# Nine pairs of an attention layer issued by another timing table, and one helper moved to the head of the queue for free slots

## The chip, the cores and the metric

The kernel runs on one core of one Trainium2 chip. The metric is device time in microseconds (us), the median of several runs; lower is better. A core has five engines that run side by side, each through its own instructions in the order in which they were issued: PE (TensorE, matrix products; its weight loads are listed apart as PEld), DVE (VectorE), ACT (ScalarE), POOL (GpSimd) and SP (SyncE, which here issues all transfers). They wait for each other through semaphores.

## The reference, cut to what matters

The reference is a two-layer transformer on 1024 latent and 256 context tokens, width 1024, 16 heads of 64. The change touches only layer 0's attention. For each head, every latent token attends to an 8 by 16 neighbourhood of the 16 by 64 grid, with a bias by relative position, and to all 256 context tokens, in one softmax; context tokens attend to the context tokens alone. The results of all heads are multiplied by `w_o`, scaled by a gate and added to the input:

```python
s_nb = q_r . k_b * scale + bias ; s_nb = where(col_in, s_nb, -1e30)
s_cx = q_r . kc * scale
p = softmax(concat([s_nb, s_cx]))
o = p[..., :n_nb] @ v_b + p[..., n_nb:] @ vc
y = o @ w_o ;  h = h + g1 * y          # g1 and five more vectors: silu(c) @ ada_w + ada_b
```

## The kernel before, in words

Every product is made from operands split in two parts (a high part, and the rest), so a projection step is three matmuls: high by high (L781), high weight by low operand (L782), low weight by high operand (L783). A weight unit of 128 x 1024 that was loaded (`wr`) has to be split before PE can use it: two ACT casts (`wh`, L693) and two subtractions on DVE or POOL (`wl`, L695), 512 columns each.

Layer 0's attention runs in two passes. Queries are cut into blocks of 128, taken two at a time; such a couple, for one head, is a **pair**. The first pass (`pairs[0]`, 48 pairs) has for each head the blocks b = 0, b = 8 (the context, a short pair) and b = 2; the second (`pairs[1]`, 32 pairs) has b = 4 and b = 6. Counted from 0 in order of issue, pairs 0 to 47 are the first pass and 48 to 79 the second. Pairs 39 to 47 are heads 13, 14 and 15 of the first pass.

A pair is a fixed set of stages. For each of its two blocks: `S` (scores with the neighbourhood, two matmuls, L1992 and L1993), `X` (scores with the context, L2010 and L2011), `m` (bias and row minimum on DVE, L2004), `mX` (the same for the context, L2015; one per pair), `mn`, `e` (exponential on ACT, L860), `sr` (reciprocal of the sum), `sc` (scaling on POOL, L871), `T` (transposes on PE, L878), `c` (high part of the transposed block, ACT, L886), `s` (its low part, DVE, L891), `PV` (product with the values, L508), `oc`, `r`, `z` (results put together and written to `Od`).

The order in which everything is issued is written out ahead by a planner on a clock of its own, in ns. A **table** gives for each stage a due time from the pair's start, and a period, the distance from one pair to the next. `ORDERA` has the period 7622, `ORDERB` 5560. Stages of all pairs are sorted by due time and issued so. The tables also hold **fill slots** for other work: a `PF` slot lets the projection at the head of a list of jobs issue matmuls (the phase's rate is added to a credit of at most 6 steps, and steps are issued until the credit is used up); an `AF`, `DF` or `GF` slot gives one ACT, DVE or POOL instruction to a helper that asks for it. Per pair `ORDERA` has 3 PF, 4 AF, 5 DF and 3 GF slots, `ORDERB` 3 PF, 2 AF, 2 DF and 2 GF. If the job at the head lacks its split weights, a PF slot issues nothing, and the credit is kept up to its cap.

Helpers stand in three lines; a free slot goes to the first helper that asks, line 0 before line 1 before line 2, and within a line by entry:

- line 0: the finishing of projections (`finish_qk0`: L823 on ACT, L825 on DVE; `out_add0`: L1899 on DVE), and the two instructions per head that make the bias;
- line 1: `weights`, which splits weight units (L693, L695), and behind it `out_split0` for b = 0, 2 and 1, which loads the written results of two heads (`o<-Od`), and splits them (L1879 on ACT, L1881 on DVE) as the operand of the output projection;
- line 2: `ada0`, which makes the gate vectors with a long multiply-and-sum on DVE (`adaj`, L503, 128 x 512).

The list of PF jobs is: the query, key and value projections that the first pass needs, then the seven query projections of the second pass (`(1, 1)` to `(7, 1)`, 24 matmuls of 512 columns each), then the output projection's eight units (`out`, 24 matmuls of 512 and 24 of 256 columns each), then the first jobs of the feed-forward part. The output projection can start for a block when `out_split0` of that block and the first part of `ada0` are done. When the plan is at its end, what is left of these jobs is issued with all slots free. Behind it the feed-forward part starts with the projection of the second half (`pf`).

Of the kernel before, what the change touches and what calls it, by code (L numbers as in the profile page):

```python
# [31 lines left out]

V_NMIX, V_NFFN, V_NFIN, V_B, V_QG, V_KG, V_C = 0, 16, 32, 40, 136, 137, 138
V_N = 154
CFG = dict(lag=3, tv=5.0, tm=5.0, t1=40.0, t2=55.0, ts=43.0, p0=28, lo="GD", n=39, ra=2.3, rc=0.7, rq=1.1, rb=1.05, gap=263, r1=1.262, lh=300, tk='ADAG', tb=1000000000.0, tg=1, lp='GD')
PERIOD1 = 8172
ORDER1 = {
# [8 lines left out]
PERIODA = 7622  # L46
ORDERA = {
# [6 lines left out]
}  # L54
PERIODB = 5560
ORDERB = {
# [6 lines left out]
}  # L63
# [9 lines left out]
def _build(tc, nc, I, O, top):  # L73
# [193 lines left out]
    def startup():  # L267

        ET = mybir.EngineType
        with ExitStack() as ph:  # L270
# [10 lines left out]
            def start(at, gen):  # L281

                heapq.heappush(todo, (at, next(count), gen))
# [17 lines left out]
            def loads():  # L301
# [12 lines left out]
                for i in range(2):  # L314
                    load_raw(f"v{i}", W[16:18, :, i * 512:i * 512 + 512])
                    start(now + CFG["tv"], split(f"v{i}", w0))
                    yield 1.5
# [38 lines left out]
            def stat(b):  # L356
                n = BLK[b][1]
                acc = []
                for kc in range(KC):
# [10 lines left out]
                    yield 0.55  # L370
                yield CFG["tm"] if b == 1 else 2.0
                ms = psp.tile([P, 512], F32, name="ms")
# [74 lines left out]
            def first_qk(b):  # L447
# [3 lines left out]
                for kc in range(KC):  # L451
                    while (b, kc) not in ready or b == 0 and min(kc + CFG["lag"], KC - 1) not in ready:
                        yield 0.2
# [20 lines left out]

            for at, gen in [(0.0, loads()), (5.0, c_rows()), (10.0, stat(0)), (CFG["t1"], stat(1)), (CFG["t2"], stat(2)), (28.0, projections())] + \
                    [(CFG["ts"], shifts_ctx())] + \
                    [(max(9.5, a), modulation(m)) for m, a in enumerate((7.0, 13.0, 18.0, 22.0, 25.0, 28.5, 31.5, 34.5))]:
# [77 lines left out]
    class Lanes:  # L555
# [170 lines left out]
        def tick(self, cost=1.0):  # L726

            self.now += 650
            for e in "TML" + CFG["tk"]:
                if self.busy.get(e, 0) < self.now + CFG["tg" if e == "G" else "tb"]:  # L730
# [1060 lines left out]
    with ExitStack() as ph:  # L1791
# [6 lines left out]
        bg = Lanes(pb)  # L1798
# [55 lines left out]
        def out_split0(b):  # L1854

            while bg.pending(*((p, b % 2) for p in range(PAIRS)), *(("v", i) for i in range(4))):
                yield ""
            c0, w = BLK[b]
            oh, ol = acts_o[b] = new_act(b)
            nxt = None  # L1860
            for kc in range(KC):
                while not set((kc, t0) for t0 in range(c0 // P, (c0 + w) // P, 2)) <= written:
                    yield ""
                o32 = pb.tile([P, w], F32, name=f"o32_{b}", bufs=1 if b == 1 else 2)
                dma(out=o32[:], in_=Od[kc][:, c0:c0 + w])
                if nxt is not None:
                    yield from nxt
                nxt = split_o(oh, ol, kc, o32, bg.now + 3000)
                if b == 1:
                    yield from nxt  # L1870
                    nxt = None
            if nxt is not None:
                yield from nxt
# [172 lines left out]
        for i, job in enumerate(bg.main[:2]):  # L2046
# [3 lines left out]
        ffn0 = Ffn(0, I["x1"], H0d, lambda m: modB[0][:, m, 0:1], lambda m, b: modB[0][:, 24 + m, which(b):which(b) + 1])  # L2050
        pairs = [[Pair0(h, ps, i) for h in range(HEADS) for i in range(3 - ps)] for ps in range(2)]
        n = CFG["n"]
        plan = Plan([(PERIODA, ORDERA, pairs[0][:n], CFG["ra"], 0), (PERIODA, ORDERA, pairs[0][n:], CFG["rq"], CFG["gap"]),
                     (PERIODB, ORDERB, pairs[1], CFG["rb"], 0)])
        load_head(0, 0)
        masks = pb.tile([P, 2, 3, P], F32, name="masks", bufs=1)
        dma(out=masks[:], in_=I["masks"])
# [7 lines left out]
        bg.enter("g1", ada0(16, 24), 0.0, 2)  # L2065
        bg.enter("ada", ada0(24, 48), 0.0, 2)
        for b in (0, 2, 1):
            bg.enter(("o", b), out_split0(b), 0.0, 1)
        plan.issue(bg, {})
        while bg.pending("out", "bias", "g1", "ada", ("o", 0), ("o", 1), ("o", 2)):  # L2070
            bg.tick()
# [410 lines left out]
    pairs = [Pair1(h, b) for blk in range(2) for h in range(HEADS) for b in (4 * blk, 4 * blk + 2)]  # L2482
    plan = Plan([(PERIOD1, ORDER1, pairs, CFG["r1"], 0)])
# [173 lines left out]
```

## Time and profile before

| what | value |
|---|---|
| median of 3 runs | 3013.57 us (3013.36 to 3020.36) |
| the profiled execution | 3018.95 us, its span 3017.1 us |
| PE, DVE, ACT, POOL busy over the span | 97%, 76%, 54%, 41% |
| pairs 39 to 47: from `mX` of pair 39 to `mX` of pair 48 | 479.5 to 547.9 us, 68.4 us |
| pairs 48 to 59 | 547.9 to 616.1 us, 68.2 us |
| pairs 60 to 78 | 616.1 to 729.0 us, 112.9 us |
| pair 79 and what is left, to the first `pf` matmul | 729.0 to 745.7 us, 16.7 us |

A busy time is the union of an engine's instructions; matmuls are pipelined, so that the distance from one start to the next tells better what PE can do than the length of one. Edges of the stretches are the starts of the `mX` instruction (L2015), of which every pair has one.

### The profile page before, as it was taken

The page shows a single profiled execution, that of the slowest core. Times are in us where ns is not written, and L with a number is a line of the kernel's source. Part 1 is how long each engine was busy: PE and PEld are TensorE (multiplying, and loading weights), DVE is VectorE, ACT ScalarE, POOL GpSimd, SP SyncE. Part 2 cuts the span into 40 slices and gives each one's busy share as a digit, 9 for nine tenths or more (in the row PEclk, how much of TensorE's full clock was granted, in tenths as well). Part 3 has the DMA queues.
Part 4 walks back from the last instruction along what each step waited for, and adds up shares of the span by engine and source line. Part 5 has one row for each costly group of instructions (what it writes and reads, how often), then busy time and mean ns, then how long its engine had stood idle before and what let it go on. Part 6 is the DMA issues. An engine that isn't in the chain of part 4 may idle for free.

```text
span 3017.1 us, 50132 instructions
## 1 busy us (share of the span) xinstructions
PE 2915.8 (97%) x16460; PEld 2503.3 (83%) x16460; DVE 2300.5 (76%) x4671; ACT 1621.0 (54%) x3739; POOL 1238.8 (41%) x1105
## 2 busy tenths in 40 slices
PE   7999998999999999999999899999999999999998
PEld 5788997888788888888888788888888878888886
DVE  7478778876798875557777588999887887776776
ACT  4345545776742222234456489899887632333444
POOL 4246556776145451121121256666643354223112
PEclk9999999999999999999999999999999999999999
DMA  7777777887545562249656523333323343224962
GB/s 268 217 223 239 227 217 230 239 244 219 187 147 188 194 225 76 93 152 324 211 192 205 164 83 95 112 98 102 107 75 127 133 140 122 102 105 149 324 217 108
DMA packets 309218, 519.03 MB, mean 172 GB/s; under 512 B 46560, under 2 KB 113248, under 8 KB 308320
## 3 DMA queue, kind: packets, MB, share of 16 engines
q1 hardware_dynamic: 308960, 515.84, 52.7%
q8 instruction: 131, 2.15, 0.3%
q14 instruction: 127, 1.04, 0.1%
HBM read 389.61 MB, written 120.18 MB: 169 GB/s over the span
## 4 chain that ended last, share of the span: by engine, by line
PE 77%; DVE 10%; DMA 4%; ACT 3%; POOL 2%; issue 2%; SPq 1%; DVEq 0%; ACTq 0%; POOLq 0%
PE pf L1472 9%; PE pf L1474 9%; PE pf L1473 9%; PE T L878 5%; PE o L508 5%; PE pf L1721 5%; PE pf L1720 5%; PE pf L1722 5%; PE ps L781 3%; PE ps L783 3%; PE ps L782 3%; PE S L2265 2%; PE S L2266 2%; DVE pT L891 1%; PE pf L1494 1%
## 5 line engine op out<-in xcount | busy, mean ns | idle before, releaser
L871 POOL TENSOR_SCALAR Pt<-Pt,rc 128x1280 f32<-128x1280 f32 (+3 forms) x288 | 298.0, 1035 | 390.3 <-ACT pT L886 144.3
L891 DVE TENSOR_TENSOR pT<-T,pT 128x256 fp32r<-128x256 f32 (+2 forms) x672 | 341.9, 535 | 34.3 <-ACT pT L886 33.8
L886 ACT CAST pT<-T 128x256 fp32r<-128x256 f32 (+2 forms) x672 | 304.5, 477 | 111.9 <-PE T L878 107.5
L878 PE MATMUL T<-ident,Pt 128*128 128x128 f32 x1952 | 302.8, 274 | 24.1 <-POOL Pt L871 23.5
L878 PEld LDWEIGHTS T<-ident,Pt 128*128 128x128 f32 x1952 | 234.7, 140 | 80.7 <-POOL Pt L871 36.9
L508 PE MATMUL o<-pT,Vt 128*128 128x256 f32 x1952 | 295.2, 289 | 2.5 <-DVE pT L891 2.5
L781 PE MATMUL ps<-ah,wh 128*128 128x512 f32 (+1 forms) x688 | 261.2, 380 | 8.0 <-ACT ah L442 4.1
L508 PEld LDWEIGHTS o<-pT,Vt 128*128 128x128 f32 x1952 | 253.8, 189 | 9.9 <-DVE pT L891 6.2
L782 PE MATMUL ps<-al,wh 128*128 128x512 f32 (+1 forms) x688 | 251.3, 365 | 3.0 <-POOL al L132 2.3
L860 ACT ACTIVATE Pt<-S,rc 128x512 f32<-128x512 f32 (+2 forms) x384 | 247.1, 654 | 9.6 <-DVE rc L852 6.4
L783 PE MATMUL ps<-ah,wl 128*128 128x512 f32 (+1 forms) x688 | 250.7, 364 | 0.0
L2257 DVE TENSOR_REDUCE nm<-S 128x1 f32<-128x512 f32 x256 | 169.7, 683 | 35.7 <-PE S L2266 34.0
L963 POOL TENSOR_TENSOR c<-c,c 128x512 f32<-128x512 f32 (+1 forms) x63 | 93.5, 1486 | 249.6 <-DVE c L966 80.4
L966 DVE TENSOR_TENSOR c<-c,c 128x512 fp32r<-128x512 f32 (+1 forms) x166 | 131.0, 803 | 46.4 <-ACT c L1448 33.7
L860 ACT ACTIVATE Pt<-X,rc 128x256 f32<-128x256 f32 x256 | 125.0, 488 | 67.9 <-DVE rc L852 55.1
L1448 ACT CAST wh<-c 128x512 fp32r<-128x512 f32 x112 | 68.8, 618 | 166.2 <-PE pf L1473 66.5
L781 PEld LDWEIGHTS ps<-ah,wh 128*128 128x128 f32 x688 | 131.4, 191 | 21.2 <-ACT ah L442 4.2
L783 PEld LDWEIGHTS ps<-ah,wl 128*128 128x128 f32 x688 | 130.9, 190 | 21.2
L1472 PE MATMUL pf<-c,wh 128*128 128x512 f32 x376 | 146.5, 390 | 0.0
L1473 PE MATMUL pf<-c,wh 128*128 128x512 f32 x376 | 146.5, 390 | 0.0
L1474 PE MATMUL pf<-c,wl 128*128 128x512 f32 x376 | 146.3, 389 | 0.0
L906 POOL TENSOR_TENSOR r<-ob 128x256 f32<-128x256 f32 x144 | 123.5, 857 | 54.7 <-ACT ob L900 53.7
(596 smaller groups left out, 9137.4 us busy)
## 6 DMA issues: line engine op xcount, KB each, us to landing
c<-in_fout SPq DMA_DIRECT2D x119, 256.0 KB, 3.9
wr<-in_wqkv SPq DMA_DIRECT2D x53, 512.0 KB, 4.8
wr<-in_adaT SPq DMA_DIRECT2D x96, 256.0 KB, 3.2
c<-in_fin SPq DMA_DIRECT2D x68, 256.0 KB, 3.0
adaw<-in_adaT SPq DMA_DIRECT2D x64, 256.0 KB, 3.9
wr<-in_wo SPq DMA_DIRECT2D x32, 512.0 KB, 4.4
wr<-in_fin SPq DMA_DIRECT2D x58, 256.0 KB, 2.7
K<-Kd SPq DMA_DIRECT2D x64, 224.0 KB, 5.2
```

Of the source, the lines that this page charges most:

```text
L508: t.matmul(o_ap, lhsT=u.V[:, kb, :], rhs=u.pT[:, i, :], start=i == 0, stop=i == len(u.blocks) - 1)
L781: t.matmul(ps, lhsT=hi[:, c], rhs=ah[:, kc, :n], start=kc == 0, stop=False)
L782: t.matmul(ps, lhsT=hi[:, c], rhs=al[:, kc, :n], start=False, stop=False)
L783: t.matmul(ps, lhsT=lo[:, c], rhs=ah[:, kc, :n], start=False, stop=kc == KC - 1)
L860: s.activation(u.Pt[:, off:off + u.wid[c]], u.S[c], AF.Exp, bias=u.min, scale=u.sign, accum_out=u.rc[:, 3 + c:4 + c])
L871: g.tensor_scalar(Pt, Pt, u.rc[:, 2:3], 1.0, ALU.mult, ALU.mult)
L878: t.transpose(T[:, i * P:(i + 1) * P], u.Pt[:, (i0 + i) * P:(i0 + i + 1) * P], ident[:])
L886: s.copy(u.pT[:, i0:i0 + n, :P], u.T[c])
L891: v.tensor_tensor(u.pT[:, i0:i0 + n, P:], u.T[c], u.pT[:, i0:i0 + n, :P].bitcast(F32), ALU.subtract)
L1472: t.matmul(ps[:], lhsT=r32(hi[:, c]), rhs=bh, start=k == 0, stop=False)
L1473: t.matmul(ps[:], lhsT=r32(hi[:, c]), rhs=bl, start=False, stop=False)
L1474: t.matmul(ps[:], lhsT=r32(lo[:, c]), rhs=bh, start=False, stop=k == 3)
```

## The change

Three numbers and one argument are changed. The nine pairs 39 to 47, which were a phase of their own with `ORDERA` and rate 1.1, become the head of the last phase, with `ORDERB`; that phase's rate goes from 1.05 to 1.12. The 263 ns that stood between the first pass and the second now stand ahead of the nine pairs. And `out_split0` is entered in line 0, where it stood in line 1; being entered ahead of every projection's finishing there, it asks first.

```diff
-CFG = dict(..., n=39, ra=2.3, rc=0.7, rq=1.1, rb=1.05, gap=263, ...)
+CFG = dict(..., n=39, ra=2.3, rc=0.7, rq=1.1, rb=1.12, gap=263, ...)
...
-        plan = Plan([(PERIODA, ORDERA, pairs[0][:n], CFG["ra"], 0), (PERIODA, ORDERA, pairs[0][n:], CFG["rq"], CFG["gap"]),
-                     (PERIODB, ORDERB, pairs[1], CFG["rb"], 0)])
+
+        plan = Plan([(PERIODA, ORDERA, pairs[0][:n], CFG["ra"], CFG["gap"]),
+                     (PERIODB, ORDERB, pairs[0][n:] + pairs[1], CFG["rb"], 0)])
...
         for b in (0, 2, 1):
-            bg.enter(("o", b), out_split0(b), 0.0, 1)
+            bg.enter(("o", b), out_split0(b), 0.0, 0)
```

What moves, at three places. The first is **DVE in head 14** (`bm` is the bias, `pT` the transposed block). Before:

```order
L891 TENSOR_TENSOR pT<-T,pT 128x2x128
L865 TENSOR_REDUCE rc<-rc 128x1
L866 RECIPROCAL rc<-rc 128x1
L891 TENSOR_TENSOR pT<-T,pT 128x3x128
L2004 ISA S,nm<-S,bm_6468 128x384
L2004 ISA nm 128x1
L852 TENSOR_REDUCE rc<-nm 128x1
L1881 TENSOR_TENSOR al_6447<-o_2_6448,ah_6446 128x256
L503 ISA adaj,rawB<-adaw,crow_1284 128x512
L503 ISA rawB 128x1
L503 ISA adaj,rawB<-adaw,crow_1282 128x512
L503 ISA rawB 128x1
```

And now, one head further on, where the same stages stand:

```order
L1881 TENSOR_TENSOR al_6430<-o_2_6567,ah_6429 128x256
L2004 ISA S,nm<-S,bm_6715 128x384
L2004 ISA nm 128x1
L852 TENSOR_REDUCE rc<-nm 128x1
L865 TENSOR_REDUCE rc<-rc 128x1
L866 RECIPROCAL rc<-rc 128x1
L891 TENSOR_TENSOR pT<-T,pT 128x2x128
L1881 TENSOR_TENSOR al_6424<-o_0_6791,ah_6423 128x512
```

The split of results (L1881) has the slots, and the `adaj` instructions (L503) are gone from here: in pairs 39 to 47 there are 5 of them where there were 16; 7 now stand in pairs 48 to 59 and 4 in pairs 60 to 78.

The second is **ACT in head 15 of the first pass** (pairs 46 and 47). Before, the finishing of a projection (L823), a cast of weights (L693) and one of results (L1879) follow each other:

```order
L823 ACTIVATE qh<-ps_6902 128x512
L693 CAST wh<-wr 128x512
L1879 CAST ah_6446<-o_2_6856 128x256
L860 ACTIVATE Pt,rc<-X,rc 128x256
L886 CAST pT<-T 128x2x128
L860 ACTIVATE Pt,rc<-S,rc 128x384
L900 COPY ob<-o 128x512
```

Now the free slots of pairs 40 to 46 hold only casts of results and the finishing of projections, and the cast of weights at the end of this piece is the first in seven pairs:

```order
L823 ACTIVATE qh<-ps_6660 128x512
L886 CAST pT<-T 128x2x128 x2
L900 COPY ob<-o 128x512
L886 CAST pT<-T 128x2x128
L860 ACTIVATE Pt,rc<-X,nm 128x256
L1879 CAST ah_6429<-o_2_6757 128x256
L886 CAST pT<-T 128x3x128
L860 ACTIVATE Pt,rc<-X,nm 128x256
L693 CAST wh<-wr 128x512
```

In pairs 39 to 47, ACT had 10 casts of weights, and has 4.

The third is **PE in the first pair of the second pass** (pair 48). Before, projection steps (`ps`) stand one or two at a time between the stages:

```order
L1992 MATMUL S<-K_7056,Qs 128x384
L1993 MATMUL S<-K_7057,Qs 128x384
L781 MATMUL ps_7103<-ah_695,wh 128x512
L782 MATMUL ps_7103<-al_696,wh 128x512
L783 MATMUL ps_7103<-ah_695,wl 128x512
L878 MATMUL T<-ident,Pt 128x128 x3
L508 MATMUL o<-pT,Vt 128x256 x5
```

Now there is no projection step in the 44 rows ahead of this one, and then six steps stand in one piece (the last three rows come six times in a run) between the second `S` and the next `T`:

```order
L878 MATMUL T<-ident,Pt 128x128 x5
L508 MATMUL o<-pT,Vt 128x256 x2
L1992 MATMUL S<-K_6957,Qs 128x384
L1993 MATMUL S<-K_6958,Qs 128x384
L781 MATMUL ps_7147<-ah_695,wh 128x512
L782 MATMUL ps_7147<-al_696,wh 128x512
L783 MATMUL ps_7147<-ah_695,wl 128x512
```

Two more steps follow in the same pair. Such pairs now are pair 48 with 24 projection matmuls, pair 50 with 21, pair 54 with 24, pair 56 with 21 and pair 58 with 18; pairs 45 to 47, 49, 51 to 53, 55 and 57 have at most three.

Projection matmuls by stretch, 512 and 256 columns wide, counted in the two orders: pairs 39 to 47 had 114 and 18, now 72 and 24; pairs 48 to 59 had 102 and 24, now 120 and 9; pairs 60 to 78 had 120 and 120, now 123 and 135; behind that 24 and 48, now 45 and 48. From the feed-forward part on, every engine's order is what it was.

More of the change, by code (lines that the diff above doesn't have):

```diff
@@ L34 @@
 V_N = 154
-CFG = dict(lag=3, tv=5.0, tm=5.0, t1=40.0, t2=55.0, ts=43.0, p0=28, lo="GD", n=39, ra=2.3, rc=0.7, rq=1.1, rb=1.05, gap=263, r1=1.262, lh=300, tk='ADAG', tb=1000000000.0, tg=1, lp='GD')
+CFG = dict(lag=3, tv=5.0, tm=5.0, t1=40.0, t2=55.0, ts=43.0, p0=28, lo="GD", n=39, ra=2.3, rc=0.7, rq=1.1, rb=1.12, gap=263, r1=1.262, lh=300, tk='ADAG', tb=1000000000.0, tg=1, lp='GD')
 PERIOD1 = 8172
```

## The prediction

> **What bounds the kernel now.** First the page: the span, the busy shares and the chain that ended last.
>
> ```profile
> span 3017.1 us, 50132 instructions
> PE 2915.8 (97%) x16460; PEld 2503.3 (83%) x16460; DVE 2300.5 (76%) x4671; ACT 1621.0 (54%) x3739; POOL 1238.8 (41%) x1105
> PE 77%; DVE 10%; DMA 4%; ACT 3%; POOL 2%; issue 2%; SPq 1%; DVEq 0%; ACTq 0%; POOLq 0%
> ```
>
> PE has the end, and the change takes no matmul away; it can only win time in which PE stands, or lose some. So the next view is that of the stretches that the change reorders: pairs 39 to 47, 48 to 59, 60 to 78, what is left up to the first `pf`, and behind it. Columns: length, busy time (instructions) of PE, PEld, DVE, ACT, POOL, granted clock, DMA share, GB/s.
>
> ```profile
> 479.50:547.90 68.40, 57.96 (x332) 46.50 (x332) 60.12 (x164) 42.89 (x126) 43.97 (x49) 1.00 0.72 222
> 547.90:616.10 68.20, 66.46 (x445) 59.50 (x446) 57.38 (x196) 55.88 (x170) 53.68 (x62) 1.00 0.89 258
> 616.10:729.00 112.90, 107.62 (x755) 97.32 (x754) 87.61 (x307) 85.19 (x260) 80.01 (x97) 1.00 0.86 242
> 729.00:745.70 16.70, 16.61 (x116) 15.01 (x115) 8.42 (x24) 8.27 (x22) 10.28 (x12) 1.00 0.40 121
> ```
>
> In the nine pairs DVE is busy for 88% of the time and PE stands for 10 us; in the second pass PE has 97% and 95%, DVE 84% and 78%. The waits of the nine pairs say the same: POOL waits for DVE's reciprocals, and PE for POOL.
>
> ```profile
> POOL Pt L871 <- DVE rc L866: 15.0, 9, 2.8
> ACT Pt L860 <- DVE rc L852: 9.9, 6, 2.5
> PE T L878 <- POOL Pt L871: 7.5, 8, 1.1
> ```
>
> What PE needs for a pair is read from starts in order of time (start, length, rows as issued):
>
> ```profile
> 726.90 0.40 PE L782 MATMUL ps<-al,wh 128*128 128x512 f32 x1
> 727.14 0.39 PE L783 MATMUL ps<-ah,wl 128*128 128x512 f32 x1
> 727.37 0.75 PE L508 MATMUL o<-pT,Vt 128*128 128x256 f32 x5
> 727.96 0.34 PE L1992 MATMUL S<-K,Qs 128*128 128x384 f32 x1
> 728.14 0.34 PE L1993 MATMUL S<-K,Qs 128*128 128x384 f32 x1
> 728.31 0.28 PE L2010 MATMUL X<-K,Qs 128*128 128x256 f32 x1
> 728.43 0.28 PE L2011 MATMUL X<-K,Qs 128*128 128x256 f32 x1
> ...
> 728.79 0.71 PE L878 MATMUL T<-ident,Pt 128*128 128x128 f32 x5
> 729.26 0.48 PE L508 MATMUL o<-pT,Vt 128*128 128x256 f32 x2
> ```
>
> A step's matmul of 512 columns takes 0.23 us from start to start, one of 256 columns 0.12, a score matmul 0.18, a transpose 0.09, a value product 0.12. A pair of b = 4 has 4 scores, 4 `X`, 10 transposes and 10 value products: 0.72 + 0.48 + 0.94 + 1.18 = 3.3 us. All else on PE there is projection.
>
> **The change part by part.**
>
> Pairs 39 to 47. PE has 42 matmuls of 512 columns fewer and 6 of 256 more: 42 x 0.23 - 6 x 0.12 = 8.9 us less. DVE's groups in this stretch:
>
> ```profile
> L503 DVE CUSTOM_DVE_ANT_0 adaj<-adaw,crow 128x512 f32<-128x512 f32 x16 | 17.0, 1062 | 0.8 <-DMA adaw<-in_adaT 0.7
> L1881 DVE TENSOR_TENSOR al<-o,ah 128x256 fp32r<-128x256 f32 x4 | 3.2, 790 | 0.0
> L825 DVE SCALAR_TENSOR_TENSOR ql<-ps,qh 128x512 fp32r<-128x512 f32 x5 | 3.5, 690 | 0.3 <-issue 0.3
> L695 DVE TENSOR_TENSOR wl<-wr,wh 128x512 fp32r<-128x512 f32 x4 | 3.1, 773 | 0.0
> L503 DVE DVE_READ_ACCUMULATOR2_ANT rawB<- 128x1 f32 x16 | 1.3, 79 | 0.0
> L114 DVE TENSOR_TENSOR modB<-rawB 128x24 f32<-128x24 f32 x2 | 0.4, 195 | 0.0
> ```
>
> 11 `adaj` of 1.06 + 0.08 us go (12.5), two splits of weights (1.5), four short sums (0.8) and one L825 (0.7); one L1881 comes (0.8). DVE's 60.1 us become 45.4, 5.0 a pair. ACT loses six casts of weights, POOL four subtractions, so neither is next. At the share that DVE reached here, 88%, the nine pairs take 45.4 / 0.88 = 51.6 us: **-16.8**. No row shows this table with little work for PE. One bound is DVE at 94%, as in its fullest window just behind the first of these pairs (14.10 of 15 us, next row): 48.3, or -20.1. The other is the 84% of the second pass: 54.0, or -14.4. I take the middle, since the same stages of the same heads gave the 88%.
>
> ```profile
> 495.00:510.00 15.00, 11.69 (x66) 8.71 (x65) 14.10 (x38) 9.59 (x30) 11.35 (x13) 1.00 0.78 244
> ```
>
> Loads: a head of the first pass has eight loads of `K`, which SP issues in one go, as here for head 15, and which are wanted two pairs later.
>
> ```profile
> 507.20 1.11 SPq L81 DMA_DIRECT2D Qs<-Qd  x2
> 511.45 5.06 SPq L81 DMA_DIRECT2D K<-Kd  x8
> K<-Kd SPq DMA_DIRECT2D x64, 224.0 KB, 5.2
> ```
>
> 5.1 us of issue and 5.2 to land are 10.3 us; two pairs at 5.7 us are 11.4, where they were 15.2. It just fits; at worst it costs 1 us for each of three heads, which the 84% covers.
>
> Pairs 48 to 59. What left the nine pairs arrives here late, and in lumps: the casts of results and the finishing of projections take nearly all of the 18 ACT slots that are left of 36, the weight units fall behind, the job at the head of PE's list has no weights, and its credit piles up to 6 steps. PE gets 18 x 0.23 - 15 x 0.12 = 2.3 us more in all, which alone is little. But five pairs now need 3.3 + 24 x 0.23 = 8.8, 8.2, 8.8, 8.2 and 7.5 us of PE, six others 3.3. In a six-step lump (4.1 us) the `T`, `PV` and next `S` queue behind it on PE; DVE, ACT and POOL have about a pair's stages in hand and then wait for these. In the light pairs DVE sets the pace, with 57.4 us plus 7 x 1.14 for `adaj`, 2 x 0.77 for weights and about -1.3 for the rest: 65.6, or 5.5 a pair. If nothing averages: 41.5 + 6 x 5.5 + 5.7 for pair 59 = 80.2 us. If the lumps were free, DVE at 88% would give 74.5. I take 78.5, nearer the first since nothing lets DVE run ahead of PE by more than the two buffers of `S` and of `T`: **+10.3**. Bounds: below, DVE at 94%, 69.8 (+1.6); above, light pairs of 6.30 us, as one took in this stretch:
>
> ```profile
> 559.38 0.69 DVE L2015 TENSOR_REDUCE nm<-X 128x2 f32<-128x512 f32 x1
> 565.68 0.69 DVE L2015 TENSOR_REDUCE nm<-X 128x2 f32<-128x512 f32 x1
> ```
>
> That is 41.5 + 6 x 6.3 + 5.7 = 85.0 (+16.8).
>
> Pairs 60 to 78: 3 and 15 matmuls more on PE, 2.5 us. DVE gets 4 `adaj`, 3 splits of weights and some sums, about 8.3 us; 95.9 of 116 us would be 83%, below what it carried in the stretch before, so PE's work covers nearly all: **+3.0**, between 2.5 and 8.
>
> What is left: 21 matmuls of 512 columns more, 4.8 us, on PE alone. Now the second half's projection starts as `pf` at 745.71, and stands at its last operand for the last pair's result:
>
> ```profile
> 745.71 0.40 PE L781 MATMUL pf<-ah,wh 128*128 128x512 f32 x1
> 751.15 0.49 PE L781 MATMUL pf<-ah,wh 128*128 128x512 f32 x1 [0.49 <-ACT ah L1879]
> 751.88 0.50 PE L782 MATMUL pf<-al,wh 128*128 128x512 f32 x1 [0.23 <-DVE al L1881]
> ```
>
> These 0.7 us are covered by the longer rest: **+4.1**, between 3 and 4.8. Behind it the order is the same on every engine, and I count it as nothing; its cover is PE's own work, which moves as a whole.
>
> One rule speaks against moving `adaj` to where POOL is busier (64% in the nine pairs, 79% behind). With POOL's subtraction beside it, one took 1.77 us, and without, 0.69:
>
> ```profile
> 500.03 1.72 POOL L695 TENSOR_TENSOR wl<-wr,wh 128x512 fp32r<-128x512 f32 x1
> 500.53 1.77 DVE L503 CUSTOM_DVE_ANT_0 adaj<-adaw,crow 128x512 f32<-128x512 f32 x1
> 511.03 0.69 DVE L503 CUSTOM_DVE_ANT_0 adaj<-adaw,crow 128x512 f32<-128x512 f32 x1
> ```
>
> The Trainium skill, "GPSIMD Engine Reference", section 1, says that GpSimd shares its SBUF interfaces with VectorE, with contention for VectorE instructions of two SBUF inputs. The rows agree; by the rule the 11 moved ones would take the mean 1.06 plus 0.15 of the 1.08 between, 0.16 us more each, 1.8 us, on an engine that is not the bound in most of that time. The sum does without it.
>
> **Sum:** -16.8 + 10.3 + 3.0 + 4.1 = +0.6 us. The profiled execution took 3018.95 us, 1.9 more than its span, and would take 3019.6. It lies 5.4 above the median of the runs, 3013.57, from which the same difference gives **3014.2 us**.
>
> **The rivals.** *The lumps average out* (faster). DVE keeps 94% through the nine pairs and the twelve behind, since stages that a lump holds up are made good in the light pair next to it: -20.1 + 1.6 + 2.5 + 4.1 = -11.9, 3001.7 us. For it: the window of 94%, and that the light pairs leave PE 2 us each to run ahead. Against it: it can run ahead by two buffers only, a lump is of 4.1 us, and in that window PE fed DVE steadily.
>
> *The light pairs keep their length* (slower). A pair of the second table is then set by its own chain from `S` over DVE, ACT, POOL and PE to `PV`, not by an engine's sum, and takes 6.0 us in the first pass and 6.3 in the second whatever PE has to do: 9 x 6.0 = 54.0 (-14.4), then +16.8, +3.0, +4.1: +9.5, 3023.1 us. It decides from light pairs of 6.2 us on. For it: pairs of 6.30 with full PE, and the nine pairs, which at 76% PE need took 7.6 each. Against it: DVE was the reason there, by the waits.
>
> *PE's clock is halved at the lumps* (slower, mostly within what can be told). Stretches in which PE did little were followed by 3.4 us at half the clock:
>
> ```profile
> 195.40:198.80 3.40, 1.17 (x12) 0.97 (x10) 3.30 (x9) 0.58 (x1) 2.31 (x3) 1.00 0.41 139
> 198.80:202.20 3.40, 3.40 (x19) 3.40 (x17) 2.13 (x8) 2.25 (x7) 1.96 (x3) 0.50 0.90 237
> 714.20:717.60 3.40, 1.85 (x12) 1.42 (x11) 1.12 (x3) 1.68 (x5) 0.81 (x1) 1.00 1.06 243
> ```
>
> 1.17 us busy of 3.4 were too little, 1.85 enough. Light pairs need 3.3 us of PE in 5.5, or 2.0 of 3.4, and those of head 15 less; some windows will fall below. If four of the five lumps begin at half the clock, each loses 1.7 us: +0.6 + 6.8 = +7.4, 3021.0 us. The Trainium skill, "TensorE: Matmul & The Clock Gate", part 1, describes this gate: windows of about 3.4 us, half the clock after an idle one. The rows agree.
>
> **How the numbers follow.** The forecast has 0.5, with its own range 3006 to 3022 (its four bounds do not all fall to one side); averaging 0.2, long light pairs 0.2, the clock 0.1. A measurement of this kernel tells about 0.3%, 9 us, from no change. Faster by more: the first rival, 0.2. Slower by more: the second and a third of the third, 0.23. The rest, 0.57, is no change. The range reaches from about the averaging case to a little beyond the long pairs: 3002 to 3025.
>
> **What would show it.** The nine pairs, from the `mX` of pair 39 to that of pair 48: 51.6 us, with PE busy for less than 90% and DVE at about 88%. Pairs 48 to 59: 78.5 us, with six light pairs of about 5.5 and five of 7.5 to 9 us; at 72 or less averaging is right, at 84 or more the chain. From pair 79 to the first `pf`: 21 us, with no wait of `pf` for L1879. No `K` wait over 1 us on PE. A clock row of 0.50 between 480 and 560 us is the third rival. I am wrong if the feed-forward part changes its length although its order does not, or if the rest after the last pair hides its 21 matmuls.

## The result, and the profile after

The changed kernel takes **3033.73 us** (median of 4 runs, 3031.37 to 3035.73) against 3016.97 us of the kernel before on the same chip (median of 4, 3013.36 to 3022.55). The ratio is 1.0057, with a 95% interval of 1.0046 to 1.0069: slower by 0.57%, where no change had been forecast, and outside the range. The profiled execution took 3031.37 us.

The page of the changed kernel (span; busy time of each engine; shares of the chain that ended last):

```profile
span 3029.5 us, 50110 instructions
PE 2918.2 (96%) x16460; PEld 2506.5 (83%) x16460; DVE 2297.0 (76%) x4674; ACT 1620.9 (54%) x3739; POOL 1241.4 (41%) x1102
PE 77%; DVE 9%; DMA 4%; ACT 3%; POOL 3%; issue 2%; SPq 1%; DVEq 0%; POOLq 0%; ACTq 0%
```

The page tells little: 12.4 us more span, and shares that hardly differ. (The medians are 16.8 us apart; the profiled execution of the kernel before lay above its median, and this one is the fastest of its four.) The stretches tell it. They are pairs 39 to 47, 48 to 59, 60 to 78, and pair 79 with what is left up to the first `pf`; the columns are length, busy time (instructions) of PE, PEld, DVE, ACT and POOL, granted clock, DMA share and GB/s.

```profile
477.50:531.60 54.10, 47.34 (x291) 41.09 (x292) 43.02 (x132) 38.89 (x116) 33.48 (x40) 0.97 0.69 210
531.60:614.70 83.10, 73.84 (x450) 62.65 (x448) 64.67 (x212) 58.59 (x176) 61.66 (x66) 0.98 0.79 233
614.70:741.10 126.40, 114.48 (x774) 103.98 (x775) 94.78 (x325) 85.54 (x264) 86.53 (x99) 0.96 0.80 230
741.10:762.22 21.12, 21.05 (x137) 18.80 (x135) 8.19 (x24) 8.66 (x23) 9.79 (x12) 1.00 0.44 140
```

Against the same rows of the kernel before, the lengths differ by -14.3, +14.9, **+13.5** and +4.4 us. What lies ahead of pair 39 is 2.0 us shorter and what lies behind the first `pf` 4.1 us shorter (3029.5 - 762.2 = 2267.3 against 2271.4), which are sizes by which these parts differ between executions of other kernels too. So the first two stretches cancel, and the loss stands in the third, where the forecast had +3.0. There PE stands for 126.40 - 114.48 = 11.9 us, where it had stood for 5.3, and it is busy 6.9 us longer, of which only 2.5 us are its 18 more matmuls; the rest goes with the granted clock of 0.96, of which more below.

The waits of pairs 50 to 78 (547 to 742 us; who waited, line, for whom: us in all, times, the longest) show what is new:

```profile
ACT ah L1879 <- DMA o<-Od: 19.9, 5, 5.8
PE T L878 <- DVE rc L852: 10.6, 6, 3.7
```

In the kernel before, the same view over 547 to 730 us (its pairs 48 to 78) has for L1879 the row below, and none for PE's wait:

```profile
ACT ah L1879 <- DMA o<-Od: 4.1, 3, 2.1
```

The cast that `out_split0` issues (L1879) waits on ACT for the load of its operand five times, 4.0 us each, where there were three waits of 1.4 us. One of the five in order of time (start, length, engine, line; in brackets the idle time before it):

```profile
614.23 0.38 SPq L81 DMA_DIRECT2D o<-Od  x1
...
617.13 0.28 PE L783 MATMUL ps<-ah,wl 128*128 128x256 f32 x1
...
619.58 0.62 ACT L1879 CAST ah<-o 128x512 fp32r<-128x512 f32 x1 [5.77 <-DMA o<-Od]
...
620.50 0.42 DVE L891 TENSOR_TENSOR pT<-T,pT 128x256 fp32r<-128x256 f32 x1 [5.11 <-ACT pT L886]
...
621.07 0.41 PE L878 MATMUL T<-ident,Pt 128*128 128x128 f32 x2 [3.66 <-DVE rc L852]
...
621.42 1.22 POOL L906 TENSOR_TENSOR r<-ob 128x256 f32<-128x256 f32 x1 [5.81 <-ACT ob L900]
```

The load is issued at 614.23 us, and the cast starts at 619.58. ACT stands for 5.8 us, that is from 613.8 us on, before the load was even issued, although casts of `T` and copies of `o` that it could do are queued behind that one cast. DVE stands for ACT's `pT` (5.1 us), POOL for its `ob` (5.8 us), and PE, after the projection steps that stood there, for 3.7 us. The chain that ended last goes through the load itself:

```profile
614.23 5.32 DMA o<-Od
...
619.58 0.02 ACT ah L1879
```

The stall is then paid for a second time, by PE's clock. Two pairs of windows of 3.40 us (columns as above):

```profile
557.18:560.58 3.40, 1.46 (x10) 0.94 (x9) 2.93 (x11) 2.42 (x9) 3.40 (x5) 1.00 0.82 252
560.58:563.98 3.40, 3.40 (x16) 3.30 (x17) 2.06 (x6) 1.94 (x5) 0.95 (x2) 0.50 0.87 262
618.62:622.02 3.40, 0.95 (x8) 0.98 (x9) 1.52 (x5) 2.44 (x7) 0.60 (x1) 1.00 1.08 258
622.02:625.42 3.40, 3.40 (x17) 3.40 (x16) 2.96 (x12) 2.43 (x9) 1.81 (x3) 0.50 0.79 200
```

In the second pair PE had 0.95 us of work while ACT waited, and the next 3.4 us ran at 0.50. Such halved windows begin at 519.6, 560.6, 622.0, 697.1 and 724.4 us, the last three behind waits of L1879. The kernel before has none between 470 and 790 us. Three times 1.7 us are, as an estimate, 5.1 us of the third stretch.

Stall and halved clock together make three long pairs, 60, 72 and 76, from `mX` to `mX`:

```profile
614.70:625.76 11.06, 7.10 (x44) 6.93 (x45) 5.41 (x20) 4.88 (x15) 3.66 (x5) 0.85 0.92 266
693.13:702.38 9.25, 6.92 (x37) 5.86 (x36) 5.23 (x20) 5.00 (x15) 4.76 (x5) 0.82 0.95 267
719.56:730.30 10.74, 7.49 (x39) 6.25 (x38) 5.21 (x20) 5.00 (x15) 4.43 (x5) 0.84 1.01 280
```

Last, the end of what is left:

```profile
762.04 0.62 ACT L1879 CAST ah<-o 128x512 fp32r<-128x512 f32 x1 [6.94 <-DMA o<-Od]
...
762.22 0.40 PE L781 MATMUL pf<-ah,wh 128*128 128x512 f32 x1
```

Here too ACT stood for its load, for 6.9 us, but PE had the products left over to do, and the row of the first `pf` shows no idle time: this wait cost nothing.

### The profile page after: what moved, and what is told of

Same layout as the page of the kernel before. It is cut to its first block, busy times and chain, and to the rows that moved or that the text cites. A ratio compares the mean times of both kernels' runs of the same rounds, so it can differ in the third digit from the quotient of the medians.

```text
span 3029.5 us, 50110 instructions
## 1 busy us (share of the span) xinstructions
PE 2918.2 (96%) x16460; PEld 2506.5 (83%) x16460; DVE 2297.0 (76%) x4674; ACT 1620.9 (54%) x3739; POOL 1241.4 (41%) x1102
## 4 chain that ended last, share of the span: by engine, by line
PE 77%; DVE 9%; DMA 4%; ACT 3%; POOL 3%; issue 2%; SPq 1%; DVEq 0%; POOLq 0%; ACTq 0%
PE pf L1474 9%; PE pf L1472 9%; PE pf L1473 9%; PE T L878 5%; PE o L508 5%; PE pf L1720 5%; PE pf L1721 5%; PE pf L1722 5%; PE ps L781 3%; PE ps L782 3%; PE ps L783 3%; PE S L2266 2%; PE S L2267 2%; DVE pT L891 1%; PE pf L1494 1%
```

## The experiments

Kernels that were run together share runs of the kernel before on the same chip. A profile is of one execution; that of the changed kernel with casts 8000 ns later is its kernel's fastest (3016.96 us, by a median of 3021.30), and that of the table for five pairs its kernel's longest (3029.20 by 3024.39). Three explanations stood to be told apart. **A**: from the first place in line the cast reaches ACT, which takes its work in order, ahead of its load. **B**: the first place loses by what it puts back, above all the splits of weights, so that projection steps come in lumps. **C**: the second table makes the loss.

### The first place alone, and the table alone

```diff
# e2_first_place_only: the kernel before, with
-            bg.enter(("o", b), out_split0(b), 0.0, 1)
+            bg.enter(("o", b), out_split0(b), 0.0, 0)
# e1_table_only: the changed kernel, with
-            bg.enter(("o", b), out_split0(b), 0.0, 0)
+            bg.enter(("o", b), out_split0(b), 0.0, 1)
```

> The kernel before with one edit: the split of results is entered in line 0 instead of line 1; tables and rates stay. Theory A (the casts L1879 of the second half's results now reach ACT before their transfer has landed, and ACT, which works in order, stands): ACT's wait for o<-Od in pairs 60 to 78 grows from 4.8 us to about 20, the stretch from 112.9 to about 125 us, the whole is 8 to 14 us slower than before. Theory B (the first place costs by starving the weights, so that projections come in lumps): here no lump arises, since the projection steps per pair are those of the kernel before; within 4 us of before. Theory C (the second table alone makes the loss): no difference, within 4 us.

> The changed kernel with the split of results in line 1 as before: the second table for the nine pairs and rate 1.12 alone. By the order the projections then keep coming through pairs 39 to 52, but pairs 53 to 62 have one lump of 24 matmuls and else nothing, because the output projection waits for the split of results, and 123 matmuls are left behind the last pair (before 72, changed 93). Theory A: no ACT wait beyond 6 us; nine pairs 54 us (-14), the hole of pairs 53 to 62 about 56 us for ten pairs at DVE's pace, no loss against before there, the rest after the last pair 28 us (+11); in all -5 to +5 us against before. Theory B: the table starves PE and costs as in the changed kernel, +10 or more. Theory C: +12 to +18.

Measured: the first place alone is **1.0066** (1.005 to 1.0081), the table with its rate alone **1.0014** (1.0004 to 1.0025). The first three stretches of the first place alone, and its waits over 548 to 744 us:

```profile
476.65:548.14 71.49, 60.43 (x334) 49.51 (x333) 61.34 (x165) 43.42 (x127) 43.62 (x48) 0.95 0.72 218
548.14:624.50 76.36, 68.81 (x445) 60.95 (x444) 58.24 (x197) 56.11 (x169) 52.34 (x61) 0.98 0.79 226
624.50:743.33 118.83, 108.56 (x756) 99.15 (x754) 86.46 (x309) 84.11 (x260) 81.82 (x97) 0.99 0.80 229
```

```profile
ACT ah L1879 <- DMA o<-Od: 23.3, 7, 5.3
```

PE has the same projection steps in every pair as in the kernel before (all but one step stand in the same pair), so here there are no lumps, and still all three stretches are longer, by 3.1, 8.2 and 5.9 us, with the casts' wait at 23.3 us in the last two. B's lumps cannot explain that. In the first stretch L1879 waits nowhere; there are two halved windows (from 506.8 and 544.3 us) and a wait of 3.0 us of a cast of weights (L693) for its load. The table alone:

```profile
481.66:537.86 56.20, 55.36 (x336) 47.83 (x337) 44.76 (x132) 40.08 (x116) 33.56 (x40) 1.00 0.75 228
537.86:610.89 73.03, 62.28 (x397) 52.87 (x395) 62.06 (x212) 57.30 (x175) 58.57 (x64) 0.98 0.87 250
610.89:723.85 112.96, 107.51 (x756) 97.81 (x757) 93.61 (x327) 86.74 (x266) 87.09 (x99) 1.00 0.85 246
723.85:753.70 29.85, 26.65 (x164) 23.66 (x163) 10.15 (x27) 8.94 (x23) 9.88 (x13) 0.94 0.42 123
```

-12.2, +4.8, 0.1 and +13.2 us: the nine pairs do become shorter, and what they no longer do comes back at the end, where 123 projection matmuls are left behind the last pair in place of 72. C is at most a small part of the loss.

### The changed kernel, with the casts asked for later

`out_split0` asks for a cast 3000 ns of the plan's clock behind the load. In two kernels the casts of the second half (b = 1), which are those that waited, come later: by 8000 ns in place of 3000, or by going back to line 1.

```diff
# e3_casts_later: the changed kernel, with
-                nxt = split_o(oh, ol, kc, o32, bg.now + 3000)
+                nxt = split_o(oh, ol, kc, o32, bg.now + (8000 if b == 1 else 3000))
# e4_second_half_in_line_1: the changed kernel, with
-            bg.enter(("o", b), out_split0(b), 0.0, 0)
+            bg.enter(("o", b), out_split0(b), 0.0, 1 if b == 1 else 0)
```

> The changed kernel, all helpers in the lines where it has them, but the cast of the second half's results is asked for 8000 ns of the planner's clock after its load, not 3000. Theory A: as with block 1 back in line 1, pairs 60 to 78 at 113 to 116 us and ACT's wait for o<-Od under 3 us, +1 to +7 us against before; if the later cast of the last result delays the second half's projection, 3 us of that come back there. Theory B and C: +15 to +18 us against before.

> The changed kernel, but the split of results for block 1 (the second half) back in line 1, those for blocks 0 and 2 in line 0. Projection steps per pair are those of the changed kernel, except for one step. Theory A: the stretch of pairs 60 to 78 falls from 126.4 to about 116 us, ACT's wait for o<-Od under 6 us; 9 to 12 us faster than the changed kernel, +3 to +8 us against before. Theory B: the lumps are still there, so no gain over the changed kernel: +15 to +18 us against before. Theory C: the same as B.

Measured: **1.0012** (0.9999 to 1.0026) with 8000 ns, 1.0028 (1.0018 to 1.0038) with line 1. Stretches two and three with 8000 ns, and then the third with line 1:

```profile
530.35:612.64 82.29, 72.55 (x450) 60.97 (x448) 64.23 (x215) 58.62 (x176) 61.31 (x66) 1.00 0.80 240
612.64:725.05 112.41, 109.43 (x774) 100.55 (x775) 93.77 (x320) 86.98 (x264) 88.22 (x101) 1.00 0.89 252
```

```profile
613.37:728.01 114.64, 110.06 (x774) 100.59 (x775) 93.98 (x322) 86.99 (x264) 86.09 (x99) 1.00 0.89 250
```

The lumps are the same as in the changed kernel, and pairs 48 to 59 keep their 82 us. Pairs 60 to 78 fall from 126.4 to 112.4 and 114.6 us. With 8000 ns no L1879 waits over 0.15 us for its load in any stretch, and there is no halved window from pair 39 to the first `pf`: in pairs 60 to 78 PE stands for 3.0 us where it stood for 11.9, and is busy for 109.4 us where it was for 114.5. Pairs 60, 72 and 76 have 6.5, 5.8 and 5.8 us, 13.0 of the 14.0 us that the stretch is shorter. With line 1 there remain 2.9 us of waits up to pair 78. A is confirmed: of the 0.57%, about 0.45 points (1.0057 less 1.0012) are the casts' wait, with the halved windows behind it.

### How late is late enough

```diff
# e7_casts_5us_later: the changed kernel, with
-                nxt = split_o(oh, ol, kc, o32, bg.now + 3000)
+                nxt = split_o(oh, ol, kc, o32, bg.now + (5000 if b == 1 else 3000))
```

> The whole change, with the casts of the second half asked for 5 us behind their load, in place of 3 (as changed) or 8 (run before: 112.4 us for pairs 60 to 78). The five idle times over pairs 60 to 78 were 3.3 to 5.8 us each, 19.9 in all. Theory A in its plain form (the plan's clock and the chip's run alike, each wait shorter by what is added): five waits of 1.3 to 3.8, about 9.9 us left, pairs 60 to 78 at 119 to 120, span 3022 to 3023, ratio about 1.003. Theory A with slots (2 us move a cast to the next place that the plan has for ScalarE, which lies some us behind): as with 8, pairs 60 to 78 at 112 to 114, ratio 1.000 to 1.002. If the wait had nothing to do with it: 126, ratio 1.0057.

Measured: **1.0008** (0.9999 to 1.0018). Pairs 60 to 78, and their waits of L1879 (531 to 742 us):

```profile
615.55:728.82 113.27, 109.54 (x774) 100.49 (x775) 94.91 (x323) 86.86 (x264) 84.80 (x99) 1.00 0.89 253
```

```profile
ACT ah L1879 <- DMA o<-Od: 1.6, 3, 0.6
```

2 us more on the plan's clock take away 18 of 19.9 us, not the 10 of the plain form, as the form with slots had it: the cast falls into a later slot of ACT. A wait of 7.4 us behind pair 79 is left, like the one of 6.9 us in the changed kernel, and PE shows no idle time there either.

### The same delay without the table, and without the first place

```diff
# e5_before_casts_later: the kernel before, e6_first_place_casts_later: with the first place alone,
# e8_table_casts_later: with the table and its rate alone; each with
-                nxt = split_o(oh, ol, kc, o32, bg.now + 3000)
+                nxt = split_o(oh, ol, kc, o32, bg.now + (8000 if b == 1 else 3000))
```

> Nothing of the change in it: the kernel before, in which only the casts of the second half (line 1879, b = 1) are asked for 8 us of the plan's clock behind their load, not 3. The kernel before has a small share of the same idle time: 4.1 us in 3 idle times of ScalarE over pairs 60 to 78, 4.8 us in 2 from pair 79 to the first `pf`. Theory A (an in-order ScalarE that is handed a cast whose load has not landed): both go; in the changed kernel 19.9 us of it cost 14.0 us of pairs 60 to 78 (126.4 against 112.4 with later casts), 0.70 us each, so that pairs 60 to 78 go from 112.9 to about 110.0, the last stretch from 16.7 to 15 to 17, and the whole to 0.999 of the time before (0.998 to 1.000). Rival (so small a wait lies wholly under TensorE's work): pairs 60 to 78 stay at 112.5 to 113.5, ratio 1.000.

> The kernel before with the first place in line for the split of results (the edit that by itself made 1.0066), and the casts of the second half asked for 8 us behind their load. Projection steps lie as in the kernel before. Theory A (all that the first place costs is the cast ahead of its load): the idle times before line 1879 (6.5 us over pairs 48 to 59, 16.8 over pairs 60 to 78, 5.7 behind) go, pairs 48 to 59 come from 76.4 to 67 to 70, pairs 60 to 78 from 118.8 to 109 to 114, and the whole to 0.998 to 1.001 of the time before. Theory B (the first place costs by what it puts back, the weights and the other steps in line): the two stretches stay above 74 and 116, ratio 1.004 or more.

> The table for the nine pairs without the first place in line (by itself 1.0014), and the casts of the second half asked for 8 us behind their load. Projection steps per pair are those of the table alone, 123 products behind the last pair. Theory A: only the 5.6 us of idle time in the last stretch can go, of which TensorE's row of products behind the last pair covers most: the last stretch from 29.9 to 27 to 30, all else as with the table alone (56.2, 73.0, 113.0), ratio 1.000 to 1.0015: the table then costs what its late products cost, and no more. Theory C (the table itself loses elsewhere): ratio above 1.0015, and a stretch other than the last is longer than before by over 6 us.

Measured, with the others as a table (ratio to the kernel before, 95% interval):

| | casts 3000 ns behind the load | casts of b = 1 8000 ns behind |
|---|---|---|
| neither | 1 | 0.9990 (0.9977 to 1.0003) |
| table and rate | 1.0014 (1.0004 to 1.0025) | 0.9990 (0.9980 to 1.0000) |
| first place | 1.0066 (1.0050 to 1.0081) | 1.0023 (1.0012 to 1.0035) |
| both (the change) | 1.0057 (1.0046 to 1.0069) | 1.0012 (0.9999 to 1.0026) |

Read across, the wait costs 0.43 and 0.45 points where the casts have the first place, and 0.10 and 0.24 where they have not. Read down on the right, the first place still costs 0.33 points without the table and 0.22 with it. With the later casts the table can't be told from nothing: 0.9990 with and without it, and 1.0012 beside 1.0023 with intervals that overlap.

In the kernel before with later casts, pairs 60 to 78 went from 112.9 to 110.9 us, a gain of 2.0 where 2.9 were expected, and the other stretches are as they were. Not all of the waits went, as had been expected: one of 0.9 us is left in pairs 60 to 78, and one of 3.4 us behind the first `pf`. The table with later casts has its last stretch at 25.3 us, below the 27 to 30 expected:

```profile
614.84:725.74 110.90, 107.15 (x756) 97.74 (x755) 87.06 (x307) 84.51 (x260) 81.49 (x97) 1.00 0.88 246
```

```profile
720.83:746.10 25.27, 25.04 (x165) 22.46 (x163) 11.01 (x27) 9.14 (x23) 9.37 (x13) 1.00 0.53 168
```

The table alone had 29.85 us there, of which PE stood for 3.2 and ran at a clock of 0.94. PE's longest idle time (3.0 us) and a halved window (from 733.4 us) follow ACT's wait of 3.65 us for the cast at 732.2 us, which I had put under PE's work. ACT's other wait there, of 1.95 us, cost PE nothing, as did one of 3.3 us that the table with later casts still has.

A's expectation for the first place with later casts (0.998 to 1.001) was missed: 1.0023. B's (1.004 or more, pairs 48 to 59 above 74 us and pairs 60 to 78 above 116) was missed too: the profile has 73.9 and 113.7 us there. That execution was the longest of its kernel (3040.75 us, by a median of 3025.49), so the kernel was run once more:

> The kernel with the first place and later casts once more (1.0023 of the time before; its profiled execution was among its longest, 3040.75 us by a median of 3025.49). Theory B's rest (the place still costs by the weights and steps that it puts back): pairs 39 to 59 longer than in the kernel before by 5 us or more, with idle time of ScalarE or GpSimd for a load of weights or K, and pairs 60 to 78 at 111 to 114. If it was that execution alone: pairs 39 to 59 within 3 us of 136.6.

That execution took 3029.85 us, its span being 3027.8. Pairs 39 to 47 and 48 to 59, and waits over both (478.7 to 622.7 us):

```profile
478.73:548.72 69.99, 60.78 (x334) 49.26 (x333) 61.26 (x166) 43.37 (x127) 43.06 (x48) 0.95 0.74 222
548.72:622.65 73.93, 68.32 (x446) 60.98 (x445) 58.01 (x196) 55.95 (x169) 52.18 (x61) 0.98 0.80 235
```

```profile
ACT ah L1879 <- DMA o<-Od: 3.3, 1, 3.3
ACT wh L693 <- DMA wr<-in_wqkv: 3.1, 1, 3.1
ACT wh L693 <- DMA wr<-in_wo: 2.4, 1, 2.4
```

143.9 us against 136.6 in the kernel before (the longest execution had 147.2), so it was not that one execution; 7.3 us longer, as B's rest had it (pairs 60 to 78, with 114.9, are just over its 111 to 114). The waits are of both kinds. The 3.3 us are A's own once more: the cast at 560.4 us is one of 256 columns, so of b = 2, which is still asked for 3000 ns behind its load. The other two are casts of weights (L693) that stand at the head of ACT ahead of their own load, in the same manner; that they do so because the first place puts the splits of weights and their loads back is argued, not tested. In the kernel before with later casts, over 478 to 615 us, the only such wait over 0.15 us is of 1.5 us. Four halved windows are in these stretches: two in pairs 39 to 47, one in pairs 48 to 59 and one in pairs 60 to 78. That these waits and the clock are all of the 0.3 points was not shown.

### Two tries at a better kernel

One has of the change only the rate (`rb` 1.12), the other the table for five pairs only (43 to 47); both have the later casts.

```diff
# e9_rate_only_casts_later: the kernel before with casts 8000 ns behind, and
-CFG = dict(..., rb=1.05, ...)
+CFG = dict(..., rb=1.12, ...)
# e10_five_pairs_casts_later: the table with casts 8000 ns behind, and
-        plan = Plan([(PERIODA, ORDERA, pairs[0][:n], CFG["ra"], CFG["gap"]),
-                     (PERIODB, ORDERB, pairs[0][n:] + pairs[1], CFG["rb"], 0)])
+        plan = Plan([(PERIODA, ORDERA, pairs[0][:n], CFG["ra"], 0), (PERIODA, ORDERA, pairs[0][n:43], CFG["rq"], CFG["gap"]),
+                     (PERIODB, ORDERB, pairs[0][43:] + pairs[1], CFG["rb"], 0)])
```

> The kernel before with the casts of the second half asked for 8 us behind their load, and of the change only the rate `rb` (1.05 to 1.12); table and place as before. Products of the projection per pair: the same up to pair 50, 12 to 12 less over pairs 51 to 57, and 39 left behind the last pair in place of 72. Theory that TensorE's work is conserved (what is left behind the last pair runs there at its own length, about 0.10 us a product as the table alone showed: 123 left for 29.9 us, 72 for 16.7): the last stretch falls from 16.5 to 10 to 13, pairs 48 to 79 grow by 1 to 4 for the 33 products moved into them, ratio 0.997 to 0.9995. Rival (in the pairs a product costs as much as behind them, or more, since it sits in an uneven row: 0, then 36): pairs 48 to 79 grow by 5 or more, ratio 0.9995 to 1.001.

> As the table with later casts (0.999), but only pairs 43 to 47 have the second pass' table, pairs 39 to 42 the first pass' table as before (rate 1.1, gap 263). Products left behind the last pair: 105 in place of 123; pairs 54 to 61 are without any but 24, as there. Theory of conserved work: pairs 39 to 47 at 61 to 64 (half of the 12.6 us that the table alone wins there), pairs 48 to 59 at 70 to 73, pairs 60 to 78 at 112 to 113, the last stretch at 21 to 24, together 266 as with nine pairs and ratio 0.998 to 1.000. Rival (the table wins time of its own where VectorE bounds the pairs, and five pairs win half of it): together 269 or more, ratio 1.0005 or more.

Measured: 1.002 (1.0011 to 1.0029) and 1.001 (1.0001 to 1.002). The rate alone: pairs 48 to 59 and the last stretch, then a cast of weights in pair 53, and the first `pf` that stood, with its cast:

```profile
548.73:624.83 76.10, 69.89 (x460) 61.15 (x461) 58.74 (x200) 55.95 (x170) 52.55 (x61) 1.00 0.80 230
...
733.65:745.55 11.90, 11.34 (x83) 10.30 (x82) 7.25 (x22) 7.75 (x21) 6.77 (x9) 1.00 0.42 130
```

```profile
584.93 0.62 ACT L693 CAST wh<-wr 128x512 fp32r<-128x512 f32 x1 [3.48 <-DMA wr<-in_wo]
...
756.70 0.62 ACT L1879 CAST ah<-o 128x512 fp32r<-128x512 f32 x1 [9.92 <-DMA o<-Od]
...
757.37 0.80 PE L781 MATMUL pf<-ah,wh 128*128 128x512 f32 x1 [6.87 <-ACT ah L1879]
```

Against the kernel before with later casts the last stretch falls by 4.6 us, as expected: 0.14 us for each of the 33 products that left it. (The expectation's 0.10 us does not follow from its own lengths, 13.2 us for 51 products or 0.26.) But pairs 48 to 59 are 7.6 us longer: 3.3 of them in pair 57, which has 36 projection matmuls behind none in pair 56, and 3.8 in pair 53, where a cast of weights stood on ACT for 3.5 us for a load issued 6.9 us earlier, and PE for 2.6. Pairs 60 to 78 are 2.1 us shorter (108.8), so that pairs 48 to 78 grow by 5.5 us, as the rival had it (its ratio of at most 1.001 was missed), and all four stretches together by only 1.0. The larger loss lies behind them. With only 39 matmuls left behind the last pair PE reaches the last load before it has landed and stands for 6.9 us, and 6.8 us at half the clock follow (755.7 to 762.5 us): the products left over had been its cover. With five pairs the sum of the four stretches is 272.2 us, over the 269 of the rival, where nine with the same casts had 266.3; a part of that is two halved windows (502.9 and 615.5 us), and whether five pairs lose by themselves stays open. No kernel here is proved faster than the one before: the two at 0.9990 have intervals that reach 1.000.

## Why the prediction was wrong, point by point

**The step that failed** is the one on pairs 60 to 78: "+3.0, between 2.5 and 8", because "PE's work covers nearly all". It measured +13.5 us. The count of matmuls and of DVE's work was right: DVE is busy for 94.8 us of the 95.9 worked out, and with later casts the stretch has 112.4 us, 1.5 more than the kernel before with the same later casts (110.9). What was left out is that moving `out_split0` to the first place also moves its own instruction on an in-order engine. The prediction costed that edit through the weights it starves, and never set the cast's new place against the load's landing. The trace of before had what was needed: L1879 was already ACT's row of waits for `o<-Od`, with 8.9 us in 5 times from 477 to 765 us, and the load took a median of 3.4 us to land against the plan's 3.0:

```profile
o<-Od SPq DMA_DIRECT2D x14, 256.0 KB, 3.4
```

These 0.4 us alone would not make waits of 4.0. On the chip the distance itself was gone. With each wait subtracted from the start of its cast, ACT in the kernel before reached the five casts of pairs 60 to 78 at 2.1 to 3.5 us after their loads' issue; in the changed kernel it reached four of them 0.1 us after the issue at the latest (three before it), and the fifth 2.1 us after. So nearly the whole landing time was waited for. SP, which issues the loads in order, had stood for 3.2, 3.1 and 3.4 us just ahead of the three loads whose casts are followed by a halved window; that this is what used up the plan's 3 us is likely, but no run tested it. The prediction read the row on PE at `pf`, saw that the longer rest covers it, which is so, and did not look for the same wait in the pairs, where nothing covers it.

**Pairs 39 to 47**: 54.1 us for 51.6, at the edge of the bounds (48.3 to 54.0). DVE needed 43.0 us, less than the 45.4 worked out (1.2 us of that since the five `adaj` left took 0.83 us each, not 1.06), and reached 80%, not 88%. So the share of DVE was the wrong measure, and that the bound by 84% came out at 54.0 is luck in part: with the true 43.0 us it would have been 51.2. Four kernels that share this order took 53.2 to 54.1 us, and little of the gap is clock: the kernel without halved windows has 53.2. The table alone, with 9 to 18 projection matmuls in eight of the nine pairs, took 56.2 with PE busy for 55.4: there PE is the bound.

**Pairs 48 to 59**: 83.1 us for 78.5, within the bounds. The starts of `mX` give the pairs:

```profile
531.63 0.69 DVE L2015 TENSOR_REDUCE nm<-X 128x2 f32<-128x512 f32 x1
540.83 0.69 DVE L2015 TENSOR_REDUCE nm<-X 128x2 f32<-128x512 f32 x1
546.62 0.69 DVE L2015 TENSOR_REDUCE nm<-X 128x2 f32<-128x512 f32 x1
554.40 0.69 DVE L2015 TENSOR_REDUCE nm<-X 128x2 f32<-128x512 f32 x1
560.13 0.69 DVE L2015 TENSOR_REDUCE nm<-X 128x2 f32<-128x512 f32 x1
567.44 0.69 DVE L2015 TENSOR_REDUCE nm<-X 128x2 f32<-128x512 f32 x1
```

9.2, 5.8, 7.8, 5.7 and 7.3 us. The five heavy pairs sum to 42.0 us for the 41.5 of "nothing averages". The six light ones have a mean of 5.9, between the 5.5 from DVE and the rival's 6.2; one of them, pair 52, is the one of 7.3, in the halved window at 560.6. (Without a halved window, in the kernel with later casts, they still have 5.8.) So nothing averaged. Of the 4.6 us that the step is off, 1.7 are the step from 80.2 down towards averaging, and the rest is mostly the light pairs. That the lumps cost is seen in the heavy pairs, which take what PE needs for them. The table alone, with 73.0 us, is no test of it: it has 75 projection matmuls in this stretch, where the changed kernel has 129.

**What is left** measured +4.4 for +4.1, with no wait of `pf`. **Behind it** the order was the same, and 4.1 us less are of the size by which that part differs between executions (2268.7 to 2279.1 in the other kernels, the longest being the one whose `pf` stood), though 1.4 below the shortest of them. **The loads of K** made PE wait nowhere by over 0.15 us from pair 39 to the first `pf`; POOL stood once for one, 4.2 us, which had no place in the forecast.

**The rivals.** Averaging is out. The long light pairs came true in part (54.1 for 54.0, 83.1 for 85.0): with 2.5 and 4.6 us they are 7.1 of the 17.9 by which the sum of the four stretches (+18.5) missed the forecast (+0.6); 10.5 are the failed step. The halved clock was right as a mechanism and wrong as to place: one window in five lies between 480 and 560 us, none begins in one of the five heavy pairs, and three follow ACT's stalls, which no rival named. None of the cases held the cause.

**The rule on GpSimd's shared interface** ("GPSIMD Engine Reference" of the Trainium skill, section 1) was weighed with 1.8 us. The direction is as the rule has it: in the changed kernel an `adaj` took 0.83 us in the nine pairs, 1.14 in pairs 48 to 59 and 1.01 in pairs 60 to 78, where POOL is busier (62%, 74% and 68%). But against the 1.06 us of the kernel before the 11 moved ones took 1.10, which is 0.4 us in all. That contention is what lengthens them was not tested.

## What to carry to other kernels

When a helper is moved forward in line, the question is not only whom it pushes back, but whether its own operand has landed by then: compare each load's measured landing time with the distance that the trace shows between the load's issue and the moment when its engine reaches the cast, not with the delay that the plan allows (here 3.0 us in the plan, and 0.1 us or less in four of five cases on the chip), and ask what is queued behind the waiting instruction on its engine. A small wait in the profile of before (here 4.1 us in three times) marked the place where an earlier slot became a stall. And work left over at the end of a stage can be the cover of a last load, so that moving it forward gains less than its length.

## What the runs showed of the hardware

ACT took its instructions in order: with casts of `T` queued behind it, one cast without its operand held the engine for 5.8 us, and within that time DVE stood for 5.1, POOL for 5.8 and PE for 3.7 us. The Trainium skill, "Perfetto Trace Analysis", in the part on the TensorE instruction, says that ACT, DVE and GPSIMD are strict FIFO; the trace agrees.

A load of 256 KB from DRAM (`o<-Od`) landed 3.5 us after its issue in the median of the changed kernel, and up to 5.3 us. The Trainium skill, "DMA: Bandwidth & Descriptors", in the anatomy of one DMA, gives a fit of 2.0 us plus the bytes over 436,000 per us for transfers issued by GpSimd, an estimate of 2.6 us for these; the measured loads, issued by SP with the DMA engines 80% busy in pairs 60 to 78, are longer, and the measurement decides.

PE's clock was halved after windows of 3.4 us with 1.46 us of work as after 0.95, so a window need not be empty for it; 1.85 us, in the kernel before, had been enough. The busy time alone does not set the limit: in the execution of 3029.85 us, 1.72 us of work in a window (497.1 to 500.5) were followed by half the clock, and 1.48 us (196.7 to 200.1) were not. The Trainium skill, "TensorE: Matmul & The Clock Gate", part 1, has half the clock after an idle window of about 3.4 us; the length agrees, while these windows were not idle, and neither was the one of 1.17 us that the prediction shows.
